# Conditioning weights by quarters, the normalised input scaled in two column parts, and the first key head one block behind the gates

## The chip, the cores and the metric

The kernel runs on one core of one Trainium2 chip. A core has a matrix engine (TensorE, PE in the profile; its weight loads are listed as PEld), VectorE (DVE), ScalarE (ACT), GpSimd (POOL) and SyncE (SP), which here only starts transfers. The metric is device microseconds of one execution; shown are the median and the spread of three.

## The reference

A two-layer backbone over 512 latent tokens and 256 context tokens with 1024 channels. Layer 0 is a bidirectional gated DeltaNet, layer 1 attention. All that matters here is how layer 0 begins:

```
shift, scale, gate = jnp.split(sc_lat @ ada_w[i] + ada_b[i], 3, axis=-1)      # and the same for the context
u_lat = rms_norm(h_lat, norm_g[i]) * (1.0 + scale[:, None]) + shift[:, None]
p = u @ w_in
```

`ada_w[0]` is 1024 by 3072: its first third of columns gives the shift, the second the scale, the last the gate. Channel block k (128 channels of the 1024) of u needs shift and scale of that block alone. The product `u @ w_in` runs over all eight channel blocks. Its columns hold queries, keys, values, a gate path, and 64 columns called `ab`, from which the recurrence's gates are made.

## The kernel before

The first 60 us are one stage in which TensorE, VectorE and ScalarE follow an order written out by hand (`tc.manual_schedule`); within it a scheduler may place instructions from later code in gaps, and it orders the transfers, which SyncE issues one after another from one queue.

The stage works as follows.

Six tiles of x (two of context, four latent; 128 tokens by 1024) are loaded, squared and summed on ScalarE (L325), and once all six sums are there and one reciprocal root is made, each tile is multiplied by its factor, alternately on VectorE (L329) and ScalarE (L331).

The conditioning weights come in blocks of 512 columns, each as two loads of 1 MB (`ada_load`, L236; rows of 2 KB). Blocks 0 and 2 are the first halves of shift and scale, 1 and 3 the second halves. Five buffers take these loads, so that the sixth waits for the first products. `ada_products` multiplies a block on TensorE (L245) and copies the result to `rows` (L246). `ada_cols` turns half of the channels, shift and scale together, into columns (L258) and makes the factors `au` in two VectorE operations (L262, L263).

`turn_x(k)` turns channel block k of all six tiles on TensorE (L341), into the two PSUM buffers of the tag "tr". `make_u(k)` multiplies by scale and adds shift: the context part on VectorE (L353), the latent part on ScalarE (L355). It then splits u in a high part (ScalarE cast, L358) and the remainder (VectorE, L359). `gemm_step(nm, ..., k)` adds block k's three products (high by high, low by high, high by low) for context and latents to the sums of `nm` (L228): once for `ab`, once for the first key head `k0`. Called a gate step and a key step here, they take 1.05 us each at the full clock.

Weights of the projection are split likewise by `load_w`: a ScalarE cast (L210) and a subtraction (L211), on VectorE for `ab`, on GpSimd for `k0` and the later key heads. A block of these weights has two raw buffers.

The order per block k was: make u(k), turn block k+1, gate step k, key step k. The products of block 1 come ahead of that at k = 1, those of block 3 at k = 2, the second columns at k = 3. Behind the stage the first key head's convolution, the gates and the other key heads follow in the scheduler's order, and later stages in the order of a planner that the change doesn't touch.

## Time and profile before

| what | value |
| --- | --- |
| median of three runs | 1182.38 us (1180.96 to 1186.59) |
| the profiled execution's own time | 1193.88 us |
| its span | 1192.1 us |
| TensorE busy | 1134.5 us, 95% |
| VectorE busy | 836.9 us, 70% |
| ScalarE busy | 705.8 us, 59% |
| GpSimd busy | 631.4 us, 53% |
| TensorE busy in the first 60 us | 38.6 us |

The profile comes from one execution, slower than the median by about 1%; differences of times are taken within it. A line of the timeline gives start and duration in us, the engine, the line of the kernel, the operation, output and inputs with partitions by elements, the count, and in brackets how long the engine stood idle before it and what ended that. A line of the chain of waits gives start, duration and what the end hung on. A line by stretch gives, after the stretch and its length, the busy time of PE, PEld, DVE, ACT and POOL with their counts of instructions, TensorE's granted clock (1.00 is full), the DMA engines' busy share and GB/s.

### The profile page before, as it was taken

The page shows a single profiled execution, that of the slowest core. Times are in us where ns is not written, and L with a number is a line of the kernel's source. Part 1 is how long each engine was busy: PE and PEld are TensorE (multiplying, and loading weights), DVE is VectorE, ACT ScalarE, POOL GpSimd, SP SyncE. Part 2 cuts the span into 40 slices and gives each one's busy share as a digit, 9 for nine tenths or more (in the row PEclk, how much of TensorE's full clock was granted, in tenths as well). Part 3 has the DMA queues.
Part 4 walks back from the last instruction along what each step waited for, and adds up shares of the span by engine and source line. Part 5 has one row for each costly group of instructions (what it writes and reads, how often), then busy time and mean ns, then how long its engine had stood idle before and what let it go on. Part 6 is the DMA issues. An engine that isn't in the chain of part 4 may idle for free.

```text
span 1192.1 us, 28134 instructions
## 1 busy us (share of the span) xinstructions
PE 1134.5 (95%) x10779; PEld 921.5 (77%) x10779; DVE 836.9 (70%) x1842; ACT 705.8 (59%) x1831; POOL 631.4 (53%) x515
## 2 busy tenths in 40 slices
PE   3999999999998999999999999999998989999996
PEld 1777678888887888888566666788886878989885
DVE  2498664778889687777678888687667866556536
ACT  5544344677666668655779888653533246666632
POOL 0031014329999899793575598557663043153531
PEclk9999999999999999999999999999999999999999
DMA  9478977555646585785988856576743021121133
GB/s 320 167 229 243 305 238 207 152 170 143 175 118 206 186 237 176 238 255 172 276 225 243 248 155 172 169 228 191 234 159 124 1 71 36 37 71 37 40 131 77
DMA packets 166104, 204.56 MB, mean 172 GB/s; under 512 B 13489, under 2 KB 115026, under 8 KB 165202
## 3 DMA queue, kind: packets, MB, share of 16 engines
q1 hardware_dynamic: 159170, 199.13, 55.0%
q10 hardware_dynamic: 6800, 3.64, 1.0%
q8 instruction: 85, 1.39, 0.5%
q14 instruction: 49, 0.40, 0.1%
HBM read 161.96 MB, written 40.67 MB: 170 GB/s over the span
## 4 chain that ended last, share of the span: by engine, by line
PE 82%; DVE 6%; DMA 6%; ACT 2%; issue 2%; SPq 1%; POOL 1%; ACTq 0%; DVEq 0%; POOLq 0%
PE g L752 29%; PE po L1385 11%; PE ks L1460 6%; PE pg L2026 3%; PE pg L1980 3%; PE g_k L414 3%; PE po L2094 2%; DMA aw<-in_ada_w 2%; PE kv L1833 2%; PE su L1515 2%; PE s L2044 2%; PE pso L2327 2%; PE pr L1485 2%; PE pa L245 1%; PE pt L2072 1%
## 5 line engine op out<-in xcount | busy, mean ns | idle before, releaser
L752 PE MATMUL g<-uh,wh 128*128 128x512 f32 (+1 forms) x640 | 222.0, 347 | 0.0
L752 PE MATMUL g<-ul,wh 128*128 128x512 f32 (+1 forms) x640 | 217.7, 340 | 3.9 <-issue 3.9
L752 PE MATMUL g<-uh,wl 128*128 128x512 f32 (+1 forms) x640 | 217.1, 339 | 0.0
L769 DVE SCALAR_TENSOR_TENSOR acc<-g,cwv,acc 128x510 f32<-128x510 f32 (+1 forms) x192 | 117.0, 614 | 43.7 <-ACT acc L761 39.2
L752 PEld LDWEIGHTS g<-uh,wl 128*128 128x128 f32 x640 | 122.8, 192 | 17.4 <-issue 4.2
L752 PEld LDWEIGHTS g<-uh,wh 128*128 128x128 f32 x640 | 122.8, 192 | 14.6 <-issue 1.1
L752 PEld LDWEIGHTS g<-ul,wh 128*128 128x128 f32 x640 | 123.0, 192 | 12.5 <-issue 0.5
L1385 PE MATMUL po<-woh,y 128*128 128x512 f32 x384 | 127.7, 400 | 0.0
L1468 POOL TENSOR_TENSOR S<-S,glb 128x512 f32<-128x512 f32 x88 | 89.9, 1041 | 58.1 <-PE ks L1460 58.1
L1052 POOL TENSOR_TENSOR X<-X,tmp 128x62 f32<-128x62 f32 (+15 forms) x93 | 95.6, 1028 | 7.3
L1051 POOL TENSOR_TENSOR tmp<-L,X 128x62 f32<-128x62 f32 (+15 forms) x93 | 94.6, 1018 | 6.4
L1460 PE MATMUL ks<-S,ckq 128*64 128x256 f32 x768 | 93.5, 386 | 2.3 <-ACT O L1465 2.2
L1385 PEld LDWEIGHTS po<-woh,y 128*128 128x128 f32 x384 | 72.2, 188 | 14.8 <-issue 0.2
L1460 PEld LDWEIGHTS ks<-S,ckq 128*64 128x64 f32 x768 | 51.1, 137 | 41.5 <-ACT O L1465 10.4
L1328 POOL TENSOR_TENSOR wol<-wo,woh 128x512 fp32r<-128x512 f32 (+1 forms) x32 | 52.6, 1643 | 56.2 <-ACT woh L1319 25.5
L1385 PE MATMUL po<-wol,y 128*128 128x512 f32 x192 | 75.1, 391 | 0.0
L743 POOL TENSOR_TENSOR wl<-w,wh 128x1024 fp32r<-128x1024 f32 x11 | 26.4, 2399 | 90.5 <-ACT wh L738 72.8
L211 POOL TENSOR_TENSOR wl_k<-w_k,wh_k 128x1024 fp32r<-128x1024 f32 x8 | 19.0, 2386 | 99.2 <-ACT wh_k L210 99.2
L761 ACT ACTIVATE acc<-g,cwv 128x512 f32<-128x512 f32 (+1 forms) x48 | 27.9, 581 | 64.2 <-PE g L752 63.7
L2075 DVE TENSOR_TENSOR pT<-pt,pT 128x384 fp32r<-128x384 f32 x64 | 33.4, 554 | 45.4 <-ACT pT L2074 45.4
L1463 DVE SCALAR_TENSOR_TENSOR r<-ks,negV,cv 128x128 f32<-128x128 f32 x192 | 56.6, 345 | 7.2 <-PE ks L1460 3.6
L1533 DVE TENSOR_TENSOR S<-su,S 128x512 f32<-128x512 f32 x88 | 56.6, 685 | 5.7 <-PE su L1515 3.9
(416 smaller groups left out, 2887.8 us busy)
## 6 DMA issues: line engine op xcount, KB each, us to landing
aw<-in_ada_w SPq DMA_DIRECT2D x24, 1024.0 KB, 7.5
w<-in_dn_w_in SPq DMA_DIRECT2D x40, 512.0 KB, 4.9
wo<-in_dn_w_out SPq DMA_DIRECT2D x32, 512.0 KB, 3.9
cv<-v_d SPq DMA_DIRECT2D x80, 128.0 KB, 5.5
df<-gc_d SPq DMA_DIRECT2D x48, 128.0 KB, 3.5
z_d<-sil SPq DMA_DIRECT2D x16, 384.0 KB, 4.3
v_d<-vt SPq DMA_DIRECT2D x16, 384.0 KB, 4.2
t_d<-Tt SPq DMA_DIRECT2D x6, 1024.0 KB, 4.7
```

Of the source, the lines that this page charges most:

```text
L414: mm = T.matmul(pg_[:m, :n], w[:, k, :m], u[:, k, c0:c0 + n], start=k == 0 and n_ == 0, stop=k == KT - 1 and n_ == 2)
L752: T.matmul(ps[:, :n], w_[:, k], u[:, k, c0:c0 + n], start=k == 0 and m == 0, stop=k == KT - 1 and m == 2)
L769: V.scalar_tensor_tensor(a_[:, c0 + lo:c0 + hi], ps[:, lo + j - 2:hi + j - 2], cwv[:, j, ct:ct + 1], a_[:, c0 + lo:c0 + hi], ALU.mult, ALU ...
L1051: G.tensor_tensor(tv, bcast(L[:, :, j + 1:, j], 3, j + 1), bcast(X[:, :, j, 0:j + 1], 2, n), ALU.mult)
L1052: G.tensor_tensor(X[:, :, j + 1:, 0:j + 1], X[:, :, j + 1:, 0:j + 1], tv, ALU.subtract)
L1328: G.tensor_tensor(wl[:, :c], w[:, :c], wh[:, :c], ALU.subtract)
L1385: T.matmul(acc[j][nh], y[i][:, j, :], ww[k][:, nh * 512:(nh + 1) * 512], start=h == 0 and x == 0, stop=h == VH - 1 and x == 2)
L1460: T.matmul(ks[r0:r0 + 64, w], kq[:, w, slot(hh), r0:r0 + 64], St[hh][:, d], start=True, stop=True)
L1463: V.scalar_tensor_tensor(r[:, 2 * j + i], ks[:, 0, i], negV[:, visit, t, h0 + i:h0 + i + 1], v[:, 2 * hh + i], ALU.mult, ALU.add)
L1468: G.tensor_tensor(St[hh], St[hh], bcast(g_, 3, P), ALU.mult)
L1533: V.tensor_tensor(St[hh], raw(sj, 0, [[512 - 1024 * j, 2], [P, 2], [1, P]]), St[hh], ALU.add)
L1980: T.matmul(pgq, uL[i][:, k, t * P:(t + 1) * P], wq[j][:, k], start=k == 0 and n_ == 0, stop=k == KT - 1 and n_ == 2)
```

## The change

First, the conditioning weights come in four quarters of 256 channels, shift and scale of a quarter as two loads of 1 MB with rows of 1 KB. The quarter's products, copy and columns follow at their own places: quarter 0 before the first turning, quarters 1, 2 and 3 within the blocks k = 1, 3 and 5. The factors are made in three VectorE operations that read PSUM. Second, each x tile is multiplied in two column parts, columns 0 to 255 at once, the rest later, between the blocks. Third, the first key head's step for block k comes after the gate step of the next block or behind the next products, so that it runs a block behind. Besides, the low part of the first key weights moves from GpSimd to VectorE, and the two constants `arow` and `dtrow` are loaded from ScalarE's queue at the start.

```diff
+        def split_high():
+            split_at[1] = S.copy(wh[:, :, :m], w[:, :, :m]).ins
+
+        def split_low():
+            split_at[0] = E.tensor_tensor(wl[:, :, :m], w[:, :, :m], wh[:, :, :m], ALU.subtract).ins
...
-        return wh, wl, split_up
+        return wh, wl, split_high, split_low
...
-        aw = {nb: ada_load(st, 0, nb) for nb in (0, 2)}
+        nc.scalar.dma_start(arow, a["dn_a_log"].rearrange("o d h -> o (d h)").partition_broadcast(P).squeeze(1))
+        nc.scalar.dma_start(dtrow, a["dn_dt_bias"].rearrange("o d h -> o (d h)").partition_broadcast(P).squeeze(1))
+
+        def ada_quarter(s):
+
+            ws = []
+            for v in range(2):
+                w = st.tile([P, KT, 256], F32, tag="aw", name=f"awq{s}{v}", bufs=5)
+                dma(w, a["ada_w"][0].rearrange("(p k) n -> p k n", k=KT)[:, :, v * D + s * 256:v * D + s * 256 + 256])
+                ws.append(w)
+            return ws
...
+        def quarter_products(s):
+
+            ps = pa.tile([P, 512], F32, tag="gq", name=f"paq{s}")
+            for v, w in enumerate(quarter.pop(s)):
+                for kh in range(2):
+                    for g in range(4):
+                        T.matmul(ps[32 * g:32 * g + 32, v * 256:v * 256 + 256], sc[:, kh * 4 + g, :], w[:, kh * 4 + g, :], start=kh == 0, stop=kh == 1, tile_position=(0, 32 * g))
+            quarter["sums", s] = ps
+
+        def quarter_rows(s):
+
+            rows = quarter["rows", s] = st.tile([P, 512], F32, tag="rows", name=f"rowsq{s}", bufs=2)
+            S.copy(rows, quarter.pop(("sums", s)))
+
+        def quarter_cols(s):
...
+            for b in range(4):
+                T.matmul(pc[:, 2 * b:2 * b + 2], rows[:, b * P:(b + 1) * P], sel[:, :, 0], start=True, stop=True)
...
+            V.tensor_tensor(pcv[:, :, 1], pcv[:, :, 1], bcast(bb[:, 1], 1, 2), ALU.add)
+            V.scalar_tensor_tensor(au[0][:, :, 1, ks], pcv[:, :, 1], 1.0, bcast(chv[:, 48 + 2 * s:50 + 2 * s], 1, 2), ALU.add, ALU.mult)
+            V.tensor_tensor(au[0][:, :, 0, ks], pcv[:, :, 0], bcast(bb[:, 0], 1, 2), ALU.add)
+
+        quarter[0] = ada_quarter(0)
         wab = load_w(w_in, 6144, 64, "ab", V, False)
-        wk0 = load_w(w_in, 8 * P, P, "k0", G, False)
+        wk0 = load_w(w_in, 8 * P, P, "k0", V, False)
+        quarter[1] = ada_quarter(1)
...
-            for t in range(NT):
-                if t % 2 == 0:
-                    V.tensor_scalar(xn[t], xn[t], ssq[:, t:t + 1], None, ALU.mult)
+
+            def scale_x(t, E, c):
+
+                if E is V:
+                    V.tensor_scalar(xn[t][:, c], xn[t][:, c], ssq[:, t:t + 1], None, ALU.mult)
                 else:
-                    S.activation(xn[t], xn[t], AF.Copy, scale=ssq[:, t:t + 1])
+                    S.activation(xn[t][:, c], xn[t][:, c], AF.Copy, scale=ssq[:, t:t + 1])
+
+            quarter_products(0)
+            early_c, late_c = slice(0, 256), slice(256, D)
+            for t in (0, 1, 2, 3, 4):
+                scale_x(t, V, early_c)
+            scale_x(5, S, early_c)
+            quarter_rows(0)
+            scale_x(0, V, late_c)
...
-            rows = [st.tile([P, 2, 512], F32, tag="rows", name=f"rows0{half}", bufs=2) for half in range(2)]
-            ada_products(0, 0, aw.pop(0), rows[0][:, 0])
             turn_x(0)
-            ada_products(0, 2, aw.pop(2), rows[0][:, 1])
             wab[2]()
-            wk0[2]()
-            aw.update({nb: ada_load(st, 0, nb) for nb in (1, 3)})
...
+            scale_x(1, S, late_c)
+            quarter[2] = ada_quarter(2)
+            quarter[3] = ada_quarter(3)
             dma(masks, a["masks"])
-            ada_cols(0, rows[0], 0)
+            quarter_cols(0)
+            wab[3]()
             gemm_open("ab")
             gemm_open("k0")
             for k in range(KT):
                 make_u(k)
+                if k == 0:
+                    wk0[2]()
+                    scale_x(2, V, late_c)
+                    wk0[3]()
                 if k == 1:
-                    ada_products(0, 1, aw.pop(1), rows[1][:, 0])
-                if k == 2:
-                    ada_products(0, 3, aw.pop(3), rows[1][:, 1])
-                if k == 3:
-                    ada_cols(0, rows[1], 1)
+                    scale_x(3, S, late_c)
+                    scale_x(4, V, late_c)
+                    scale_x(5, S, late_c)
+                if k % 2 == 0 and k > 0:
+                    gemm_step("k0", *wk0[:2], P, k - 1)
                 if k + 1 < KT:
                     turn_x(k + 1)
                 gemm_step("ab", *wab[:2], 64, k)
-                gemm_step("k0", *wk0[:2], P, k)
-                if k == 2:
+                more = k // 2 + 1 if k % 2 == 1 and k < 7 else None
+                if more:
+                    quarter_products(more)
+                    quarter_rows(more)
+                if k % 2 == 1:
+                    gemm_step("k0", *wk0[:2], P, k - 1)
+                if more:
+                    quarter_cols(more)
+                if k == KT - 1:
+                    gemm_step("k0", *wk0[:2], P, k)
+                if k == 4:
                     pv2 = pa.tile([P, 512], F32, tag="gq", name="pv2")
```

8 lines of the change are left out of this document (6 added, 2 removed).

## The prediction

> **What bounds the kernel now.** I read the page's first block, then the chain of waits over the first 120 us, the busy time by stretch, the timeline of the first 64 us instruction by instruction, and the groups by shape of the same stretch. The page:
>
> ```profile
> span 1192.1 us, 28134 instructions
> PE 1134.5 (95%) x10779; PEld 921.5 (77%) x10779; DVE 836.9 (70%) x1842; ACT 705.8 (59%) x1831; POOL 631.4 (53%) x515
> ```
>
> TensorE is the bound of the whole. The chain shows the first 60 us, the only stretch that the diff touches:
>
> ```profile
> 9.42 13.93 DMA aw<-in_ada_w
> 23.39 1.06 PE pa L245 x8
> ...
> 54.93 0.66 PE px L341 x6
> 55.59 1.03 PE g_ab L228 x6
> 56.62 1.05 PE g_k L228 x6
> ...
> 58.73 1.07 PE g_k L228 x6
> ```
>
> To 25 us it waits for conditioning weights, at the end it is pure TensorE: 0.66 us of turnings and two steps of 1.05 us (gates, first key head) per block of 128 columns. The last step ends at 59.8. What follows decides whether a shift there reaches the end:
>
> ```profile
> 60.00:70.00 10.00, 10.00 (x73) 8.52 (x70) 9.08 (x18) 5.45 (x11) 4.42 (x2) 1.00 1.03 335
> 70.00:80.00 10.00, 10.00 (x82) 7.39 (x82) 9.79 (x29) 4.35 (x7) 2.40 (x1) 1.00 0.49 138
> 80.00:100.00 20.00, 19.79 (x146) 14.54 (x147) 19.50 (x58) 8.76 (x21) 4.26 (x2) 1.00 0.78 255
> ```
>
> The first busy column is TensorE, the third VectorE: TensorE has no slack behind the stage, so I carry a shift of the stage's end to the kernel's end in full.
>
> **The change, part by part.** The start, from the timeline:
>
> ```profile
> 2.13 0.45 ACTq L298 DMA_DIRECT2D sel<-in_sel  x1
> 3.24 1.28 ACT L316 ACT_TABLE_LOAD   x1 [3.24 <-DMA cc<-in_c_ctx]
> 7.47 1.06 ACT L325 ACTIVATE junk<-x 128x1024 f32<-128x1024 f32 x1 [0.92 <-DMA x<-in_ctx]
> ...
> 15.37 1.94 PE L245 MATMUL pa<-aw,sc 128*32 128x512 f32 x8 [10.27 <-DVE rs L189]
> 16.21 3.23 ACT L331 ACTIVATE x<-x,ssq 128x1024 f32<-128x1024 f32 x3 [2.45 <-DVE ssq L190]
> 16.21 2.08 DVE L329 TENSOR_SCALAR x<-x,ssq 128x1024 f32<-128x1024 f32 x3
> 17.99 1.58 PE L245 MATMUL pa<-aw,sc 128*32 128x512 f32 x8 [0.68 <-DMA aw<-in_ada_w]
> ...
> 24.52 0.58 ACT L246 COPY rows<-pa 128x512 f32<-128x512 f32 x1 [4.29 <-PE pa L245]
> 25.62 1.04 ACT L210 CAST wh_k<-w_k 128x1024 fp32r<-128x1024 f32 x1
> 25.66 0.69 DVE L211 TENSOR_TENSOR wl_ab<-w_ab,wh_ab 128x512 fp32r<-128x512 f32 x1 [7.37 <-ACT wh_ab L210]
> 26.65 0.17 DVE L262 TENSOR_TENSOR au<-pc,chv 128x16 f32<-128x16 f32 x1 [0.29 <-PE pc L258]
> 26.75 2.34 POOL L211 TENSOR_TENSOR wl_k<-w_k,wh_k 128x1024 fp32r<-128x1024 f32 x1 [26.31 <-ACT wh_k L210]
> 26.85 2.25 DVE L263 SCALAR_TENSOR_TENSOR au<-au,chv 128x8 f32<-128x8 f32 x1
> 29.83 1.51 PE L341 MATMUL px<-ident,x 128*128 128x128 f32 x6 [3.22 <-DVE u L353]
> ```
>
> Two constants move to ScalarE's queue: two issues of 0.45 us after the one at 2.13 end at 3.5, 0.25 us past the table load's start. It is hidden by the squares, which wait for x (0.92 us at 7.47); without that cover it costs 0.25.
>
> First quarter: as many bytes as the first old block, in its place, but in pieces of 1 KB, not 2 KB. Rates:
>
> ```profile
> 8.00:10.00 2.00, 0.00 (x0) 0.00 (x0) 0.00 (x0) 1.77 (x4) 0.00 (x0) 1.00 1.03 422
> 14.00:16.00 2.00, 0.63 (x4) 0.23 (x8) 1.67 (x10) 0.00 (x0) 0.00 (x0) 1.00 1.06 390
> 24.00:26.00 2.00, 2.00 (x22) 1.61 (x15) 0.34 (x1) 1.48 (x3) 0.00 (x0) 0.98 1.06 255
> 26.00:28.00 2.00, 0.61 (x4) 0.52 (x3) 1.67 (x3) 0.67 (x1) 1.25 (x1) 0.50 1.00 370
> 28.00:30.00 2.00, 0.17 (x1) 0.20 (x2) 1.65 (x2) 0.78 (x1) 1.08 (x1) 0.50 0.43 123
> 32.00:34.00 2.00, 2.00 (x10) 1.27 (x8) 1.43 (x4) 1.11 (x3) 0.00 (x0) 0.81 1.05 408
> ```
>
> The last column is GB/s: 422 while x moves (4 KB pieces), 390 with 2 KB, 255 with projection weights of 256 and 512 B. Per piece on one of 16 engines that is 155 and 84 ns for the first two; a line through them gives 48 ns at 1 KB, 338 GB/s: 3.1 us per MB where it was 2.7. So the second half lands at 18.8 (bounds: 18.0 if nothing is lost, 20.8 at 255 GB/s). The Trainium skill (DMA: Bandwidth & Descriptors, Specifications) names 512 B as the least size for line rate; by it the quarter lands at 18.0 and the end is 0.8 us earlier. The row at 255 has half its bytes in 512 B pieces and speaks for a loss.
>
> Durations for what comes next, from the same timeline:
>
> ```profile
> 38.93 1.07 PE L245 MATMUL pa<-aw,sc 128*32 128x512 f32 x8
> 41.78 1.05 ACT L210 CAST wh_k<-w_k 128x1024 fp32r<-128x1024 f32 x1 [3.25 <-DMA w_k<-in_dn_w_in]
> 44.66 1.95 PE L258 MATMUL pc<-sel,rows 128*128 128x2 f32 x16
> 54.77 0.82 PE L341 MATMUL px<-ident,x 128*128 128x128 f32 x6
> 55.19 0.54 DVE L353 TENSOR_SCALAR u<-px,au 128x256 f32<-128x256 f32 x1
> 55.63 0.78 ACT L355 ACTIVATE u<-px,au 128x512 f32<-128x512 f32 x1 [1.16 <-PE px L341]
> 56.30 0.91 ACT L358 CAST uh<-u 128x256 fp32r<-128x256 f32 x2
> 56.73 1.21 DVE L359 TENSOR_TENSOR ul<-u,uh 128x256 fp32r<-128x256 f32 x2 [1.00 <-ACT uh L358]
> 59.71 0.31 PEld L457 LDWEIGHTS ptab<-ident,abc 64*64 64x64 f32 x8 [0.36 <-ACT wh_k L210]
> ```
>
> The early parts of x (256 columns) cost VectorE 0.27 each and end at 17.6, x0's late part at 18.2: all under the wait for the second half, and nothing but a few tenths of us if that landed at 18.0. From there, with 0.05 us between engines and 0.1 ahead of TensorE: last products 1.07 (19.9), copy 0.58 (20.5), columns, half of the 1.95 us block, 1.0 (21.6), three small VectorE operations of 0.2 (22.25). Before, these factors stood at 29.1, of which 2.1 were lost as VectorE's 0.17 us operation took 2.25 exactly while GpSimd worked on wl_k (26.75 to 29.09); the split moves to VectorE and the new operation reads PSUM, so this stall goes. **The head start is 6.9 us.**
>
> Then in order of the new code. VectorE: wl_ab 0.69 (22.9), context u 0.54 (23.5); ScalarE's casts of u (0.91 the two) end at 24.45, VectorE's low parts at 25.2; ScalarE's cast of the key weights (1.04) ends at 25.5; x2's late columns 0.60 (25.8; 2.08/3 a tile for 1024 columns); wl_k0 at 128x1024 1.35, twice the 0.69 (27.1). It sits ahead of the second u: context u 27.1 to 27.7, ScalarE's casts to 28.65. Only behind those stand x3's and x5's late columns, 0.88 each (3/4 of 3.23/3, and 0.07 fixed): 30.4. Turning block 2 needs column 256 of every x, so TensorE stands, but for turning 1 and one gate step (2 us), **from 21.6 to 30.5**. The late x is late next: 30.5 against the old wait's end at 29.8. By then the new order is one turning and one gate step ahead, half a column block and half the products behind.
>
> The half clock of 26 to 32 (0.50, then 0.81) followed a sparse stretch like this one, so it may come again; on the work right behind 30.5 (0.44 of turning, 1.05 of gate step, taking twice as long) it costs 1.5 us if it lasts to 33, nothing if it is over. The Trainium skill (TensorE: Matmul & The Clock Gate, Part 1) lets the clock fall after an idle window of 3.4 us; by it the emptier 25.8 to 30.5 brings the half clock and the stage ends at 64.05.
>
> From the last turning (55.59) to u's last low part (57.94) pass 2.35 us. In the old order a gate step, a key step and a turning, 2.76, cover that. In the new order key steps go in pairs around the columns, so between a pair's two blocks stand only a gate step and a turning, 1.71. A pair, counted from its columns' end: key step to 1.05; factors at 0.65, context u 1.24, latent u 1.44; turning 1.34 to 2.0; casts to 2.36, low parts 2.27 and 3.10; gate step in pieces to 3.67; second context u behind the low part 3.10 to 3.64, turning 3.74 to 4.40, casts to 4.61, low parts to 5.35, gate step to 5.92; products 1.08, key step 1.05, columns 0.95: 9.0 us with 7.55 of work, **1.45 idle**. Blocks 4 and 5 carry the convolution weights' turning (0.35) and its VectorE copy, which stands ahead of a u: 10.45. Blocks 6 and 7 come to 8.0 (5.9 of work). Blocks 1 to the second columns: 0.44+1.05+1.08+1.05+0.95 = 4.6.
>
> **Sum:** 30.5+4.6+9.0+10.45+8.0 = 62.55; 64.05 with the half clock. I take the middle, 63.3, for neither row decides the clock: 3.5 behind 59.8. Off that 0.3, since the copies of the gates now lie under two key steps and the 0.36 us at 59.71 goes. Net +3.2: span 1192.1 to 1195.3. The profiled execution lies 11.5 us above the median of 1182.38 (its own time is 1193.88); I carry the difference over: **1185.6**. With hand-offs at nothing and 2 KB rates the stage ends at 60.3 (+0.3); both bounds are in the range. The last quarter's second load waits for a buffer until the second products (34.6 at the latest); behind it on SyncE may stand the next key weights, needed at 64, and that hides it.
>
> **The rivals.**
> First, *not slower*: the head start carries. If the late x come before the second u's casts end, or hand-offs are shorter than my 0.05 to 0.1 us, the work left from 30.5 without idle is 4.6+7.55+7.9+5.9 = 26.0: 56.5, with half of the 6.1 of stalls (1.45+2.55+2.1; half is 3.0) and no half clock 59.5, less 0.3: -0.6; with turning 2 at 28.5, -2.6: 1180. For it: 6.9 us of head start and the stall removed. Against: the 1.71 against 2.35, and ScalarE's place for x3 and x5.
> Second, *clearly slower*: ScalarE's cast of the next key weights is not in the hand-written order and already landed inside it at 41.78, with 3.25 us of waiting for its load. The loads are no faster now; set ahead of the third u (37.3) it holds ScalarE until 42.8, 5.5 us: 1191. Decided by whether ScalarE reaches it before the load. Against: it hid before, and there are later gaps. GpSimd's low part behind it could hold a VectorE operation for 2.3 us more.
> Third, part of the delay is swallowed: VectorE is 91 to 98% busy behind the stage; if it sets the pace there, what counts is that the gates' work begins one key step (1.05) earlier relative to TensorE: +2.1, 1184.5. Against: the gate steps themselves end later (two key steps ahead of the stage's end: 60.45 to 61.95, against 58.73).
>
> **How the numbers follow.** Forecast 0.50, first rival 0.21, second 0.13, third 0.16. I call 0.5% (5.9 us) what can be told from no change. Faster than 1176.5 needs a stage end at 53.9, below the 56.5 without idle: 0.05, a quarter of the first rival. Above 1188.3: the second rival and a tail of the forecast, 0.14. The rest, 0.81, is no change. The range takes in the first and half of the second rival: 1178 to 1190.5; the forecast's own is 1182.5 to 1187.5.
>
> **What would show it.** Right: factors ready near 22.3; TensorE idle of 4 us or more ending near 30.5 behind a scaling of x; gaps of 0.1 to 0.4 us in front of gate steps from block 2 on; last key step near 63. Wrong: turning 2 before 28, gapless blocks from 2 on, or an order after 60 us that moves by itself.

## The result, and the profile after

The changed kernel takes 1197.80 us (median of four runs, 1194.87 to 1198.48) against 1184.08 us for the kernel before (four runs, 1180.96 to 1186.59). The ratio is 1.0105 with a 95% interval of 1.0079 to 1.0131: 12.4 us slower (9.4 to 15.5); the two medians lie 13.7 us apart. Forecast were 3.2 us more, and the range ended at 1190.5.

The first lines of the page of the profile after:

```profile
span 1192.8 us, 28283 instructions
PE 1136.8 (95%) x10843; PEld 921.7 (77%) x10843; DVE 825.5 (69%) x1856; ACT 706.1 (59%) x1832; POOL 632.0 (53%) x514
```

The two spans, 1192.1 before and 1192.8 now, hide the loss: the profiled execution of the kernel before (1193.88) lies 9.8 us above the median of its timed runs, that of the changed one (1194.87) 2.9 below its median. How much of that lies behind the stage shows in the run d_exp below: its later code is that of before, the row shown next stands within 0.2 us of its place there, and its span is 1184.3. So the comparison is made inside the traces, at the end of the stage and at one row of later, unchanged code. That row, from the timeline of ScalarE, before and after:

```profile
252.29 0.47 ACT L761 ACTIVATE acc<-g,cwv 128x256 f32<-128x256 f32 x1 [0.98 <-PE g L752]
```

```profile
263.47 0.47 ACT L829 ACTIVATE acc<-g,cwv 128x256 f32<-128x256 f32 x1 [0.98 <-PE g L820]
```

The changed kernel is 11.2 us late there, about what the timed runs say. It is already late by that much when the stage ends (71.00 in place of 59.78). That the two numbers agree is partly luck: between the stage's end and that row TensorE waits 3.35 us in the changed kernel and 1.17 us before, and for the same 1500 matmuls it is busy 189.1 us in place of 191.3.

The timeline of the changed kernel's stage (start, duration, engine, line, operation, in brackets the idle time ahead and what ended it):

```profile
2.63 0.44 ACTq L311 DMA_DIRECT2D arow<-in_dn_a_log  x1
2.79 3.66 SPq L309 DMA_DIRECT2D x<-in_x  x4
3.46 0.34 ACTq L312 DMA_DIRECT2D dtrow<-in_dn_dt_bias  x1
...
13.85 1.06 ACT L373 ACTIVATE junk<-x 128x1024 f32<-128x1024 f32 x1 [0.16 <-DMA x<-in_x]
...
19.81 1.93 PE L331 MATMUL paq<-awq,sc 128*32 128x256 f32 x16 [0.97 <-DMA awq<-in_ada_w]
...
24.38 0.15 DVE L350 TENSOR_TENSOR au<-pcq,chv 128x4 f32<-128x4 f32 x1
...
25.46 0.88 PE L399 MATMUL px<-ident,x 128*128 128x128 f32 x6 [1.40 <-ACT u L413]
...
30.26 1.76 ACT L381 ACTIVATE x<-x,ssq 128x768 f32<-128x768 f32 x2
...
31.24 1.30 PE L399 MATMUL px<-ident,x 128*128 128x128 f32 x3 [1.32 <-ACT x L381]
...
34.39 3.12 PE L331 MATMUL paq<-awq,sc 128*32 128x256 f32 x32
...
38.60 0.95 PE L344 MATMUL pcq<-sel,rowsq 128*128 128x2 f32 x8
...
40.16 1.05 ACT L216 CAST wh_k<-w_k 128x1024 fp32r<-128x1024 f32 x1 [1.98 <-DMA w_k<-in_dn_w_in]
...
41.28 2.35 POOL L217 TENSOR_TENSOR wl_k<-w_k,wh_k 128x1024 fp32r<-128x1024 f32 x1 [40.84 <-ACT wh_k L216]
...
42.21 2.31 DVE L417 TENSOR_TENSOR ul<-u,uh 128x256 fp32r<-128x256 f32 x2 [1.60 <-ACT uh L416]
...
43.97 0.48 PE L234 MATMUL g_ab<-ul,wh_ab 128*64 128x256 f32 x1 [1.26 <-DVE ul L417]
...
48.20 1.93 PE L331 MATMUL paq<-awq,sc 128*32 128x256 f32 x32
...
51.21 0.95 PE L344 MATMUL pcq<-sel,rowsq 128*128 128x2 f32 x8
...
62.26 0.95 PE L344 MATMUL pcq<-sel,rowsq 128*128 128x2 f32 x8
...
70.61 0.39 PE L234 MATMUL g_k<-uh,wl_k 128*128 128x512 f32 x1
```

The last key step ends at 71.00, where it ended at 59.78. The rows to keep in mind are the start (x's issues take 3.66 us), the scaling of x at 30.26 with TensorE waiting behind it, and the cast at 40.16, which belongs to the next key head and stands between the third factors and the third u.

In the kernel before, the same issue and the last square:

```profile
2.80 1.83 SPq L303 DMA_DIRECT2D x<-in_x  x4
...
12.61 1.06 ACT L325 ACTIVATE junk<-x 128x1024 f32<-128x1024 f32 x1 [0.15 <-DMA x<-in_x]
```

Last, busy time by stretch of the changed kernel (PE, PEld, DVE, ACT, POOL, then granted clock, DMA share, GB/s):

```profile
24.00:26.00 2.00, 0.60 (x6) 0.54 (x6) 1.46 (x5) 1.16 (x3) 0.00 (x0) 1.00 1.09 348
26.00:28.00 2.00, 1.92 (x10) 0.97 (x7) 1.84 (x4) 2.00 (x4) 0.00 (x0) 0.65 1.11 341
...
34.00:36.00 2.00, 2.00 (x18) 0.79 (x20) 0.00 (x0) 0.00 (x0) 0.00 (x0) 0.50 1.09 348
36.00:38.00 2.00, 2.00 (x24) 1.07 (x17) 0.00 (x0) 0.41 (x1) 0.00 (x0) 0.79 1.12 338
...
44.00:46.00 2.00, 2.00 (x7) 1.36 (x8) 1.43 (x4) 0.93 (x2) 0.00 (x0) 0.50 0.46 111
```

By the shares of the mixed stretches (0.65 is 0.6 us at full and 1.4 at half) the clock is halved from about 26.6 to 36.8, and a second time in a spell that holds all of 44 to 46 (43.7 to 47.1 by stretches of 1 us); before, it was halved once, from 26 to 32.8.

One thing this column doesn't show. It lists 1.00 from the start, but the first products of the stage run at half speed: 16 instructions take 1.93 us at 19.81, where 32 take 1.93 at 48.20, and in the kernel before 8 take 1.94 at 15.37 and 1.07 at 38.93. In the changed kernel full speed comes at about 23 us. Ahead of the first halving the clock is therefore read from the durations.

### The profile page after: what moved, and what is told of

It is laid out like the page before. It is cut to its first block, busy times and chain, and to the rows that moved or that the text cites. A ratio compares the mean times of both kernels' runs of the same rounds, so it can differ in the third digit from the quotient of the medians.

```text
span 1192.8 us, 28283 instructions
## 1 busy us (share of the span) xinstructions
PE 1136.8 (95%) x10843; PEld 921.7 (77%) x10843; DVE 825.5 (69%) x1856; ACT 706.1 (59%) x1832; POOL 632.0 (53%) x514
## 4 chain that ended last, share of the span: by engine, by line
PE 74%; POOL 7%; DVE 7%; DMA 6%; ACT 3%; issue 2%; SPq 1%; POOLq 0%; ACTq 0%; DVEq 0%
PE g L820 21%; PE po L1453 11%; PE ks L1528 6%; PE pg L2094 3%; PE pg L2048 3%; PE g_k L482 3%; PE su L1583 2%; POOL tmp L1119 2%; PE po L2162 2%; PE kv L1901 2%; PE s L2112 2%; POOL X L1120 2%; PE pr L1553 2%; PE pso L2395 2%; PE pq L1575 1%
## 5 line engine op out<-in xcount | busy, mean ns | idle before, releaser
L1119 POOL TENSOR_TENSOR tmp<-L,X 128x62 f32<-128x62 f32 (+15 forms) x93 | 98.8, 1063 | 6.4
L217 POOL TENSOR_TENSOR wl_k<-w_k,wh_k 128x1024 fp32r<-128x1024 f32 x7 | 16.8, 2404 | 117.9 <-ACT wh_k L216 117.9
L2167 POOL TENSOR_TENSOR yT<-ay,yT 128x256 fp32r<-128x256 f32 x16 | 11.8, 738 | 91.3 <-ACT yT L2166 91.3
```

What stands on the lines that cost most here:

```text
L1119: G.tensor_tensor(tv, bcast(L[:, :, j + 1:, j], 3, j + 1), bcast(X[:, :, j, 0:j + 1], 2, n), ALU.mult)
```

## The experiments

Each run is judged by three numbers: where the last key step of the stage ends, how far the later ScalarE row (252.29 in the kernel before) has moved, and the ratio of the timed runs. The first two come from one trace each; the ratio's interval is about 0.2 to 0.5% to each side; so what differs by a few us at the stage's end cannot always be told apart in the ratio.

| run | last key step ends | later row moves | ratio, 95% interval |
| --- | --- | --- | --- |
| before | 59.78 | 0 | 1 |
| changed | 71.00 | +11.2 | 1.0105 (1.0079 to 1.0131) |
| a_const_back | 71.44 | +8.2 | 1.0108 (1.0060 to 1.0155) |
| a_no_hoist | 67.90 | +11.5 | 1.0103 (1.0058 to 1.0148) |
| a_whole_x | 69.42 | +7.3 | 1.0103 (1.0065 to 1.0142) |
| a_key_not_behind | 75.97 | +15.9 | 1.0153 (1.0108 to 1.0198) |
| a_fill | 71.00 | +9.0 | one time, 1192.95 us |
| a_fill_cast_held | 66.58 | +4.3 | 1.0081 (1.0050 to 1.0111) |
| a_three_undone | 63.41 | +2.0 | 1.0034 (1.0008 to 1.0059) |
| b_quarters | 64.88 | +4.8 | 1.0051 (1.0020 to 1.0082) |
| b_key_behind | 60.92 | -2.4 | 0.9975 (0.9953 to 0.9998) |
| b_low_on_V | 61.49 | +1.4 | 0.9988 (0.9959 to 1.0016) |
| b_const_early | 60.02 | +1.0 | 1.0002 (0.9982 to 1.0021) |
| c_low_const | 67.60 | +7.5 | 1.0040 (1.0023 to 1.0057) |
| c_low_const_fill | 66.43 | +6.6 | 1.0082 (1.0051 to 1.0114) |
| d_exp | 59.73 | -0.2 | 1.0013 (0.9992 to 1.0034) |
| d_key_exp | 60.91 | -2.4 | 0.9988 (0.9962 to 1.0015) |
| d_low_key_exp | 60.37 | -2.7 | 0.9984 (0.9963 to 1.0006) |

Names with a_ are the changed kernel with parts taken back or added, the others the kernel before with parts of the change.

### One part taken back at a time

The two constants back on SyncE's queue:

```diff
-        nc.scalar.dma_start(arow, a["dn_a_log"].rearrange("o d h -> o (d h)").partition_broadcast(P).squeeze(1))
-        nc.scalar.dma_start(dtrow, a["dn_dt_bias"].rearrange("o d h -> o (d h)").partition_broadcast(P).squeeze(1))
...
+            dma(arow, a["dn_a_log"].rearrange("o d h -> o (d h)").partition_broadcast(P).squeeze(1))
+            dma(dtrow, a["dn_dt_bias"].rearrange("o d h -> o (d h)").partition_broadcast(P).squeeze(1))
             dma(masks, a["masks"])
```

> The changed kernel with the two constants arow and dtrow back on SyncE's queue, where they were (ahead of the masks). In the changed kernel the issue of the four latent x tiles took 3.66 us where it took 1.83, the DMA engines stood half idle from 6 to 8 us, and the last square started at 13.85 instead of 12.61. Theory: two issues on ScalarE's queue with 128 pieces of 128 B each hold up SyncE's. Then the last square is back at 12.6, the scaling of x starts at 16.2 instead of 17.45, and the last key step ends 1.2 us earlier than 71.0. Rival: the 1 KB pieces behind x fill the queue; then x stays at 13.85 and the stage's end does not move.

Measured, the timeline's rows of the same two places:

```profile
2.81 2.09 SPq L309 DMA_DIRECT2D x<-in_x  x4
...
12.88 1.06 ACT L371 ACTIVATE junk<-x 128x1024 f32<-128x1024 f32 x1
```

x is back by 1.0 us, and the late scaling ends at 30.84 in place of 32.02. The stage's end does not follow (71.44): the clock is then halved from 25.3 to 35.5 and again from 42.3 to 49.2, and the next key head's casts stand in the third u as before.

The later key heads' casts held back until the stage's last cast of u:

```diff
         def split_up():
-            split_at[1] = S.copy(wh[:, :, :m], w[:, :, :m]).ins
+            with tc.issue_after(last_cast[0]):
+                split_at[1] = S.copy(wh[:, :, :m], w[:, :, :m]).ins
...
-                    S.copy(uh[:, k, c0:c0 + w_], u32[:, :w_])
+                    last_cast[0] = S.copy(uh[:, k, c0:c0 + w_], u32[:, :w_]).ins
```

> The changed kernel with the later key heads' weight casts on ScalarE held behind the stage's last cast of u, so that none is placed inside the stage. Theory: in the changed kernel the cast at 40.16 waited 1.98 us for its load and took 1.05, GpSimd's low part behind it held VectorE's low part of u for 1.1 us, and TensorE's clock fell again from 44 to 47; without it the stage ends 2 to 3.5 us earlier than 71.0, at 67.5 to 69. Against that the second key head's weights are ready only after the stage: its first product may start up to 2 us behind the last key step. Rival, the chain of u alone sets the blocks' pace: under 1 us gained.

The timeline's rows of the third u's low part, and of a later cast:

```profile
41.08 1.21 DVE L419 TENSOR_TENSOR ul<-u,uh 128x256 fp32r<-128x256 f32 x2 [0.56 <-ACT uh L418]
...
77.56 1.05 ACT L218 CAST wh_k<-w_k 128x1024 fp32r<-128x1024 f32 x1 [1.46 <-DMA w_k<-in_dn_w_in]
```

The low part takes 1.21 again, not 2.31, the two blocks from the second columns' end to the third's take 9.59 us in place of 12.61 with the clock full throughout, and the stage ends 3.1 us earlier. But two raw buffers serve all key heads: what is cast late frees its buffer late, and the fourth key head's weights wait for their load until 77.56 (their cast is at 70.81 in the changed kernel, where GpSimd is done with the buffer at 43.6 and the load is issued at 43.66; here it is issued from 67.78 on). The later row stands at +11.5: between 88 us and that row TensorE waits 3.7 us for a VectorE operation on the gates and 2.5 us for later conditioning weights. So the gain is given back behind the stage; that the late buffer brings these waits about is likely, but not shown.

x scaled whole, all of it ahead of the first turning's use:

```diff
-            early_c, late_c = slice(0, 256), slice(256, D)
-            for t in (0, 1, 2, 3, 4):
-                scale_x(t, V, early_c)
-            scale_x(5, S, early_c)
+            for t in range(NT):
+                scale_x(t, S if t % 2 else V, slice(0, D))
```

> The changed kernel with every x tile scaled at once, as before, instead of in two column parts. Theory: VectorE and ScalarE stood idle from 19 to 22 us, so the whole scaling costs nothing there, and TensorE no longer waits for late columns until 31 to 32: turning 2 starts near 28, the stage ends 2.5 us earlier than 71.0 from that alone, 4 us with less of the half clock. Rival, the half clock is set by the sparse stretch before it and the chain of u by its own latency: under 1 us.

The third turning starts at once at 28.5 and the clock is full again from 30.2 (36.8 in the changed kernel), but the cast now falls into the third u at 40.31, and TensorE stands 1.79 and 2.07 us behind it. 1.6 us are left of the gain.

The key step right behind its gate step again:

```diff
-                if k % 2 == 0 and k > 0:
-                    gemm_step("k0", *wk0[:2], P, k - 1)
...
-                if k % 2 == 1:
-                    gemm_step("k0", *wk0[:2], P, k - 1)
+                gemm_step("k0", *wk0[:2], P, k)
...
-                if k == KT - 1:
-                    gemm_step("k0", *wk0[:2], P, k)
```

> The changed kernel with the first key head's step right behind the gate step of the same block, as before. The prediction's step says that key steps in pairs leave the chain of u uncovered, 1.45 us a pair and 6.1 in all; if that is the cause, the stage ends 3 to 5 us earlier than 71.0. Rival: with the factors coming by quarters the wait only moves in front of the gate step behind each quarter's columns, where nothing is left to cover it; then the end is within 0.8 us of 71.0, and the gate steps end about 1 us later than the 68.8 of the changed kernel.

The view of waits of TensorE over this run's stage (in all, times, longest):

```profile
PE px L399 <- DVE u L411: 4.2, 4, 1.2
PE g_ab L234 <- DVE ul L417: 1.9, 1, 1.9
```

It is 5.0 us worse, which neither the theory nor the rival had, and the clock is halved three times (39.7 to 49.9, 56.8 to 60.2, 70.4 to 73.8). The wait of 1.9 is the next head's cast again. With quarters there are four columns, and behind each the chain of factors, u and PSUM buffer stands open for 1.2 us unless a key step lies over it. So the key head a block behind is no loss in this order, it covers part of a loss that the quarters bring.

### Two covers of one loss

Full clock by 24 added transposes in TensorE's empty places; their result isn't used:

```diff
             quarter_cols(0)
+            fill(8)
...
                 gemm_step("ab", *wab[:2], 64, k)
+                if k == 0:
+                    fill(16)
```

> The changed kernel with 24 idle turnings of x's first block added on TensorE where it stood idle, 8 behind the first quarter's columns and 16 behind the first gate step; their result is not used. Theory of the clock: the half clock from 27 to 37 comes from the sparse stretch ahead of it; with the filler the granted clock stays at 1.00 there, and the last key step ends 2 to 4 us earlier than 71.0 in spite of the added work. Rival: the clock falls all the same, or the waits set the pace whatever the clock; then the end stays or moves later by up to 2 us.

TensorE is at half speed until about 27.6 and at full speed from there to 44.8 us (halved again until 48.2), and the stage ends at 71.00 to the hundredth. The timeline says why:

```profile
39.90 1.04 ACT L216 CAST wh_k<-w_k 128x1024 fp32r<-128x1024 f32 x1 [0.55 <-DMA w_k<-in_dn_w_in]
...
41.28 2.97 DVE L417 TENSOR_TENSOR ul<-u,uh 128x256 fp32r<-128x256 f32 x2 [2.17 <-ACT uh L416]
...
43.71 0.33 PE L234 MATMUL g_ab<-ul,wh_ab 128*64 128x256 f32 x1 [2.07 <-DVE ul L417]
```

Everything arrives 1.5 us earlier and waits for the cast, which waits for its load, which lands at about 40 whatever TensorE does; then GpSimd's low part (41.02 to 43.37) holds VectorE's. Both treated at once, with the casts held only until the fourth block's casts of u:

```diff
             with tc.issue_after(last_cast[0]):
                 split_at[1] = S.copy(wh[:, :, :m], w[:, :, :m]).ins
...
                 if k == 3:
                     last_cast[0] = cast.ins
```

> The changed kernel with both suspects treated at once: 24 transposes more, whose result nobody reads, in TensorE's empty places of the stage (as in the run with the filled gaps, where the clock stayed at 1.00 until 44 us and the stage's end did not move from 71.0), and ScalarE's casts of the later key heads held until the fourth block's casts of u. Constants, column parts of x and the key head a block behind stay as the change has them. Theory, clock and cast are two covers of one loss, and each alone leaves the other in place: the last key step ends at 64.5 to 67, and the kernel lies at 1.003 to 1.007 of the kernel before. Rival, the cast is the only thing and the clock costs nothing: 67.9, as with the cast held alone. Second rival, a load that lands late sets the pace whatever is done: still 69.5 to 71.

66.58: 4.4 us, where the filled gaps alone brought none and the held cast alone 3.1. The theory holds for the stage; for the whole (1.0081, expected 1.003 to 1.007) it was too hopeful.

Constants, x whole and the cast held, all three, quarters and the order of the change kept:

```diff
-        nc.scalar.dma_start(arow, a["dn_a_log"].rearrange("o d h -> o (d h)").partition_broadcast(P).squeeze(1))
...
-            early_c, late_c = slice(0, 256), slice(256, D)
...
+                scale_x(t, S if t % 2 else V, slice(0, D))
...
+            with tc.issue_after(last_cast[0]):
+                split_at[1] = S.copy(wh[:, :, :m], w[:, :, :m]).ins
```

> The changed kernel with three things undone at once: the constants back on SyncE's queue, every x tile scaled whole, and the second key head's cast held until the fourth block's casts of u (not until the stage's end, which took 3.4 us back later by delaying the next weights). Quarters, the key head a block behind and the low part on VectorE stay. Theory: the terms add up; the stage ends at 62.5 to 65 (71.0 in the changed kernel, 59.8 before), the whole is 5 to 8 us below the changed kernel and still 2 to 5 us above the kernel before, since the blocks wait for each quarter's columns. Rival: quarters themselves gain, and the end is at or below 59.8.

63.41. TensorE runs at half speed until about 30.4, by the durations of its matmuls, and at full speed from there to the stage's end. Taken back alone, the three move the stage's end by -0.4, 1.6 and 3.1 us (4.3 in all), together by 7.6: each was standing in front of another. Where the 3.6 us left come from is the question of the runs below.

### Parts of the change on the kernel before

Quarters alone, the rest as before:

```diff
-        aw = {nb: ada_load(st, 0, nb) for nb in (0, 2)}
+        quarter[0] = ada_quarter(0)
...
+        quarter[1] = ada_quarter(1)
```

> The kernel before with the quarters alone: x scaled whole, key step right behind the gate step, key low part on GpSimd ahead of the columns, constants on SyncE. Theory: columns four times instead of twice, each in front of two blocks, cost more than the earlier first factors give: the stage ends at 63 to 66 (59.8 before). Rival: the quarters are the gain and the other parts the loss: 55 to 59.

```profile
PE px L394 <- DVE u L406: 5.4, 5, 1.2
```

That row of TensorE's waits holds one wait behind each of the four columns (23.5, 34.8, 45.0, 57.1) and one of 0.57. The kernel before has 3.22 and 0.48 us of waits behind its first columns, so the waits are only a part of the 5.1 us; one more quarter's products (1.93) lie behind the first columns, the clock is halved once more, from 58.7 to 62.1, and the rest isn't told apart. In the order before there were two columns, and the second came a block ahead of its need, with a gate step and a key step over it.

The low part of the key weights on VectorE, behind the first u:

```diff
-        wk0 = load_w(w_in, 8 * P, P, "k0", G, False)
+        wk0 = load_w(w_in, 8 * P, P, "k0", V, False)
...
+                if k == 0:
+                    wk0[3]()
```

> The kernel before with one thing of the change: the first key weights' low part on VectorE behind the first u, not on GpSimd ahead of the factors. Theory: VectorE's factor operation no longer stands 2.1 us behind GpSimd; factors at 27.0 instead of 29.1, the stage ends 1.5 to 2.2 us earlier than 59.8, the whole 1.5 to 2 us below the kernel before. Rival: the added 1.2 us on VectorE delays the second block's u by as much, or the half clock lasts longer; under 0.8 us.

```profile
30.74 0.23 ACT L518 ACTIVATE arow<-arow 128x32 f32<-128x32 f32 x1 [2.87 <-DMA arow<-in_dn_a_log]
...
31.32 0.47 PE L234 MATMUL g_ab<-uh,wh_ab 128*64 128x256 f32 x1 [2.01 <-ACT uh L364]
```

The factors stand at 27.07, 2.0 us earlier, and nothing comes of it: an exponential of a constant row, placed between u and its casts, waits for its load.

Nor can the 2.0 us be put down to the move. In the run with the key head behind (below) GpSimd has the low part ahead of the factors, as before:

```profile
26.77 0.17 DVE L263 SCALAR_TENSOR_TENSOR au<-au,chv 128x8 f32<-128x8 f32 x1
26.95 2.35 POOL L211 TENSOR_TENSOR wl_k<-w_k,wh_k 128x1024 fp32r<-128x1024 f32 x1 [26.50 <-ACT wh_k L210]
```

The factor operation takes 0.17, for it is done when GpSimd begins. It is so in b_const_early, d_exp and d_key_exp too. In the trace of the kernel before VectorE waited 0.29 us for the first columns, which took 2.22 us in place of 1.95, since the clock had fallen during them; in the four others it waited for nothing. So GpSimd began at 26.75, ahead of that operation at 26.85. The stall of 2.1 us is thus a matter of a tenth of a microsecond in one execution, not a property of the kernel; where it is missed, u's first low part can meet GpSimd's instead (2.13 in place of 1.21 in d_exp).

Moving those loads behind the squares on ScalarE's queue was meant to mend the wait for the row, and with 16 added transposes, whose result isn't used, to keep the clock up:

```diff
             rsqrt(ssq, 1.0 / D)
+            nc.scalar.dma_start(arow, a["dn_a_log"].rearrange("o d h -> o (d h)").partition_broadcast(P).squeeze(1))
+            nc.scalar.dma_start(dtrow, a["dn_dt_bias"].rearrange("o d h -> o (d h)").partition_broadcast(P).squeeze(1))
...
+            fill(6)
```

> The kernel before, with its two whole-block loads and x scaled whole, and two edits: the low part of the first key weights on VectorE behind the first u (in place of GpSimd), and the two constant rows on ScalarE's queue behind the squares of x, so that the exponential of the first row does not wait for its load between u and u's casts (2.87 us of wait with the low part moved alone, where the last key step ended at 61.49). Theory, the stall removed is worth what the factors gain once nothing new waits: factors near 27.1, no wait for the row, last key step at 57.5 to 58.5, kernel at 0.997 to 0.9995. Rival, the longer emptiness in front of the third half block brings the half clock for longer and eats it: last key step at 59.5 to 61, kernel at 0.999 to 1.002.

> The same two edits, and 16 transposes more whose result nobody reads, in TensorE's empty places around the second half block's products and behind the first columns, to keep the clock up. Theory, the half clock of 26 to 32 us is the rest of the loss: granted clock 1.00 from 24 on, last key step at 55.5 to 57.5, kernel at 0.995 to 0.999. Rival, the transposes themselves stand ahead of products that are due, or the loads of the weights set the stage's pace: last key step at 58 to 61, kernel at 0.999 to 1.003.

Both missed altogether. ScalarE's timeline of the first:

```profile
23.58 0.35 ACTq L333 DMA_DIRECT2D arow<-in_dn_a_log  x1
24.31 0.36 ACTq L334 DMA_DIRECT2D dtrow<-in_dn_dt_bias  x1
24.72 3.23 ACT L339 ACTIVATE x<-x,ssq 128x1024 f32<-128x1024 f32 x3 [10.75 <-DMA w_ab<-in_dn_w_in]
```

The first issue, due behind the last square (14.0), went out at 23.58, and ScalarE's scaling of x, whose factors stood at 16.4, began at 24.72; the trace puts the wait down to the landing of the `ab` weights. The stage ended at 67.60 and 66.43. These runs say nothing of the theory, but much of what an issue on a computing engine's queue can cost. The same two loads at the start, where the change has them, and nothing else:

> The kernel before with the loads of the two constant rows moved to ScalarE's queue at the start, as the change has them, and nothing else. Theory: SyncE's four issues of the latent tiles of x take 3.0 to 3.7 us in place of 1.83, the last square ends 1.0 to 1.3 us later (13.6 to 13.9), and since the first columns wait for weights the factors come 0 to 1.2 us later: last key step at 59 to 61, kernel at 0.999 to 1.002. Rival (what the prediction costed): hidden by the squares, last square at 12.6, and the exponential, whose row is there, waits for nothing: last key step at 58.5 to 59.8, kernel at 0.998 to 1.000.

```profile
2.79 3.44 SPq L303 DMA_DIRECT2D x<-in_x  x4
...
14.24 1.06 ACT L327 ACTIVATE junk<-x 128x1024 f32<-128x1024 f32 x1
```

SyncE's four issues take 3.44 in place of 1.83 and the last square starts 1.6 us later; the factors come at 28.36, earlier than the 29.10 of the kernel before only because they miss the 2.1 us described above. The stage's end moves by 0.24, the whole by nothing that can be measured. In the order before, then, an x late by 1.6 us is covered.

The key step a block behind, in the order before:

```diff
-                gemm_step("k0", *wk0[:2], P, k)
+                if k:
+                    gemm_step("k0", *wk0[:2], P, k - 1)
+                if k == KT - 1:
+                    gemm_step("k0", *wk0[:2], P, k)
```

> The kernel before with one edit: the first key head's step runs one block of 128 columns behind the gates' step. The run that took this part out of the changed kernel ended 5.0 us later, so there it covers the chain from turning to u's low part. Theory, in the order of before that chain is covered already (no idle time in front of gate steps from 54.9 on), so nothing is to be had: last key step at 59.5 to 60.1, gates' last step 1.0 us earlier (57.7), kernel at 0.9985 to 1.001. Rival, the key step behind fills the idle that stands ahead of the first gate step too: last key step at 57 to 59 and the kernel at 0.996 to 0.9985.

```profile
249.89 0.47 ACT L764 ACTIVATE acc<-g,cwv 128x256 f32<-128x256 f32 x1 [0.98 <-PE g L755]
```

The last key step ends 1.1 later, the gates' last step 0.1 later (58.83), and the later row stands 2.4 us earlier. From the stage's end to that row TensorE is busy 188.97 us without a wait, where the kernel before has 191.34 us for the same matmuls and 1.17 of waits; 2.3 of the difference lie in the products of later conditioning weights (L245: 16.8 in place of 19.1). That this comes from the gates' sums, complete a key step before the end, is a reading that no run isolates. Neither theory had that place. At 0.9975 this kernel looks slightly faster than the one before, and so than both; its interval only just leaves out 1, and d_key_exp below, with the same two numbers, has 0.9988 and an interval that holds 1.

Three more on the same ground, with the exponential held behind the fourth block's casts: alone, with the key head behind, and with the low part on VectorE besides.

```diff
-    S.activation(arow, arow, AF.Exp)
+    with tc.issue_after(last_cast[0]):
+        S.activation(arow, arow, AF.Exp)
```

> The kernel before with the exponential held behind the fourth block's casts of u, and nothing else. Theory: in the kernel before the factors come late (29.1) for the 2.1 us that GpSimd's low part holds VectorE, and the row's load lands at about 30.7, so the exponential costs at most 0.5 to 1.5 us there: last key step at 58.3 to 59.8, kernel at 0.9975 to 1.0005. Rival: nothing stands behind the exponential in this order, last key step at 59.8 within 0.1.

> The kernel before with the key head's step a block behind, and the exponential held behind the fourth block's casts; the low part stays on GpSimd. With the key head behind alone the factors stood at 26.9, but u's casts waited behind the exponential until 31.1. Theory: first gate step at 28.5 to 29.5 in place of 31.5, last key step at 58 to 59.5, kernel at 0.993 to 0.997. Rival: the factors fall back to 29.1 (VectorE's operation held by GpSimd's low part, as in the kernel before), and the hold gains nothing: first gate step at 31.5, kernel at 0.996 to 0.9995.

> The kernel before (whole-block weights, x scaled whole, constants on SyncE's queue) with the order of the change otherwise: low part of the first key weights on VectorE behind the first u, key head's step a block behind the gates' step; and ScalarE's exponential of a constant row held behind the fourth block's casts of u, so that it cannot stand between u and its casts. It is the changed kernel with three parts taken back, less the quarters. Theory, the quarters are what is left of the loss (+5.1 alone; +3.6 with these two parts): last key step at 57 to 60, gates' last step at 55 to 58, kernel at 0.993 to 0.998 of the kernel before. Rival, the order itself costs: last key step at 62 to 64, kernel at 1.002 to 1.005.

The hold alone ends within 0.1 of the kernel before, as its rival said; the other two end at 60.91 and 60.37, later than their theories had it.

In the last of them the first gate step begins at 28.01, 3.0 us ahead of the trace of the kernel before, and the clock is full from 32 on. It has whole blocks in place of quarters, and its stage ends at 60.37, its gates at 58.27, where the run with three parts taken back has 63.41 and 61.30: **the 3 us left come with the quarters.** Three smaller things differ besides. The key steps follow one by one, where the quarters' columns make them go in pairs; the exponential is held only here, which alone moves nothing; the next head's cast is held only there, but in neither run does a gate step wait for it. Quarters and pairs are not told apart by these two runs. But the stage doesn't end earlier than before either. Its timeline shows the bound:

```profile
33.76 1.06 PE L252 MATMUL pa<-aw,sc 128*32 128x512 f32 x8 [1.69 <-DMA aw<-in_ada_w]
...
40.00 1.07 PE L252 MATMUL pa<-aw,sc 128*32 128x512 f32 x8 [1.27 <-DMA aw<-in_ada_w]
```

The last conditioning weights are there at 40.0; in the kernel before and in b_key_behind, b_const_early, d_exp and d_key_exp their products wait for them too and begin between 40.4 and 40.7. From there to the end it is TensorE's work. The 3 us gained ahead are waited away in front of these loads (1.69 and 1.27). None of the three is measurably faster than the key head behind alone.

What the quarters, with the key steps in pairs, do to a gate step shows in two pairs of rows, first and last of one step's six, in the run with three parts taken back (third block):

```profile
36.77 0.36 PE L236 MATMUL g_ab<-uh,wh_ab 128*64 128x256 f32 x1
...
38.14 0.40 PE L236 MATMUL g_ab<-uh,wl_ab 128*64 128x512 f32 x1
```

and in the one with whole blocks (sixth block; its third takes the same):

```profile
52.14 0.36 PE L235 MATMUL g_ab<-uh,wh_ab 128*64 128x256 f32 x1
...
53.03 0.39 PE L235 MATMUL g_ab<-uh,wl_ab 128*64 128x512 f32 x1
```

1.37 from first to last start against 0.89: the step comes in pieces, as u's low parts get ready. The six steps of blocks 2 to 7 (counted from 0) take 8.5 us together against 5.3, which is 3.2 us.

## Why the prediction was wrong, and where it was right

The sign was right; the size was not, and anything above 1188.3 had been given only 0.14. Its stage was 30.5 + 4.6 + 9.0 + 10.45 + 8.0 = 62.55. The trace, by the ends of the columns (39.55, 52.16, 63.21) and the late x at 32.02, has 32.02 + 7.53 + 12.61 + 11.05 + 7.79 = 71.00. The 8.45 us between are 1.5, 2.9, 3.6, 0.6 and -0.2. The steps that failed, in the order of their size, are the second rival's cast, which was left out of the sum (3.0 in the third term), the quarters' products, priced at one load for two (0.85 in each of three terms), the half clock (about 2.1 in the second term), and the constants called hidden (1.2 in the first term); the rest of the working was 0.4 too long. Step by step:

- **Late x, 30.5.** The mechanism was right: TensorE waits for a scaling of x on ScalarE. It ended 1.5 later, and 1.2 of that is the step "two constants move to ScalarE's queue ... hidden by the squares". The prediction costed ScalarE's own time (0.25) and looked at no other queue; what was paid is SyncE's, whose issues doubled (1.83 to 3.66). With the loads back the late scaling ends 1.2 earlier (30.84). The run with this move alone shows the like, 3.44 and the late square, though there it costs the kernel nothing.
- **"Last products 1.07" and "products 1.08".** Mis-sized, measured 1.93. The row of 1.07 is one load of 1 MB; a quarter has two, and the row of the kernel before that holds two says so:

```profile
34.17 1.92 PE L245 MATMUL pa<-aw,sc 128*32 128x512 f32 x16
```

That is 0.85 too little in every one of three later quarters. Ahead of the first factors the 1.07 was meant for the second load alone, and it took 1.93 for another reason: it ran at half speed, as the 1.94 and 1.58 for one load each in the prediction's own rows at 15.37 and 17.99 could have told. These 0.86 us, a landing 1.0 later (19.81 for 18.8; 18.79 with the constants back) and a turning that went ahead of the columns brought the first factors at 24.53, not 22.25. The rate of 338 GB/s for pieces of 1 KB was good: 341 and 348 in the stretches above.
- **Half clock, 0 to 1.5.** It came, sooner and for longer, from 26.6 to 36.8: the second quarter's products took 3.12 in place of 1.93, and of the 2.9 us by which the blocks to the second columns exceed 4.6, 0.85 are the products' size, 1.2 their half clock, and the rest, about 0.9, lies in the gate step, which took 2.27 at half clock, less what had been turned before. A second spell, 43.7 to 47.1, lies in the next pair and goes when the cast is held. The prediction took a middle between two ends where it had no row; the upper end was too low, since the spell ended only at 36.8, when TensorE had been without a gap since 31.2. How much of that is luck the last section says.
- **A pair in 9.0.** Measured 12.61. The run with three parts taken back has 9.61 for the same pair (columns' ends 34.97 to 44.58), 11.03 for the next and 7.80 for the last: the working with its uncovered chain from turning to low part held within 0.6, and that is the missing 0.85 less a little. The other 3.0 are the **second rival**, the hoisted cast, at the place named, the third u: with the casts held and all else as in the changed kernel the pair takes 9.59, and the second half-clock spell is gone. Its price was put at 5.5 by a load landing at 41.8, and it landed at 40.16. "GpSimd's low part behind it could hold a VectorE operation for 2.3 us more" came too: 2.31 in place of 1.21.
- **"Key steps go in pairs", so the chain lies open.** Half right. It does lie open, but only together with the quarters: with whole blocks and the key head behind, where the key steps needn't go in pairs, gate steps are whole (0.89). With quarters, putting each key step right behind its gate step costs 5.0 more. The prediction compared with the old order and never priced the wait behind each of four columns, 1.2 us, which the key steps cover.
- **The head start of 6.9 us, the removed stall in it.** 4.6 came (24.53 in place of 29.10), and the late x used it up, as the prediction had it. But 2.1 of the 6.9 were that one execution's, as four other traces show. And in the order before nothing could have been had from it: there is a second bound at 40 us, the landing of conditioning weights. The prediction saw it neither as a bound nor as a rival; in the trace of the kernel before it is the idle of 0.48 at 40.48, so small because the stall had used up the rest.
- **The third rival** pointed at the right place: with the key head behind, 2.4 us are gained behind the stage, by a way that isn't shown. In the changed kernel TensorE's work there shrinks by about as much (189.1 for 191.3), but its waits grow by 2.2. So the shift of the stage's end was carried to the later row in full by luck, and not since TensorE had no slack there.

The cases were weighed as if one of them would come true. They came together. The clock fell before TensorE waited for the late x (26.6 against 29.9), and in the run with x whole it fell too, at 26.8, but came back at 30.2; so the late x lengthens the half clock and doesn't bring it. The third u then meets a load that lands near 40 us: at full clock ahead of it (39.90), with x whole (40.31), and in the changed kernel (40.16). The Trainium skill (SBUF - State Buffer, the two separate sides) says that VectorE's operation with two SBUF inputs and GpSimd exclude each other for a whole instruction; the trace agrees (GpSimd's low part runs from 41.28 to 43.63, and VectorE's, begun at 42.21, ends at 44.52, which leaves 0.9 us behind GpSimd of its usual 1.21). The moved low part of the first key head removed that at 27 us, and VectorE met it at 42 with the next head's.

Not settled: how the 7.6 us that three parts bring together divide among them. They cover each other, and the single runs give an order of undoing, not shares. Nor are quarters and key steps in pairs told apart, or the way by which a key head behind shortens TensorE's work after the stage.

## What to carry to other kernels

Before a gain ahead of a wait is counted, look for the next thing that arrives at a fixed time, a load above all: with whole blocks, three runs (the ones with the exponential held) that brought the first gate step 3 us forward all met the same load at 40 us. A constant's load moved to another engine's queue has two prices, the other queues' issues and that engine's computation behind it, and both are read in the rows of the issues, not in their bytes. Where undoing one part brings nothing, undo two before calling it harmless. And before a stall in one trace is counted as a gain, look at how narrowly it came about: the 2.1 us behind GpSimd hung on 0.1 us, and a second trace of nearly the same kernel doesn't have them.

## What the runs showed of the hardware that was not expected

Two small loads issued from ScalarE at 2.63 and 3.46 us, between SyncE's issues of x, lengthened these from 1.83 to 3.66 us in the changed kernel and to 3.44 with that move alone; with the loads back, 2.09. An issue from ScalarE due at 14.0 went out at 23.58. The trace names a load's landing for that wait; in the same trace an issue of SyncE that began at 19.87 was done at 23.36, 0.2 us ahead. Which of the two it was wasn't tried.

The clock fell in the changed kernel at about 26.6 us, with no idle stretch of TensorE longer than the 1.40 us up to 25.46 in the five us ahead of it, and it held through a gap of 1.69 us in d_low_key_exp (32.07 to 33.76; the products behind it take 1.06, as at full clock). The Trainium skill (TensorE: Matmul & The Clock Gate, Part 1) ties the fall to an idle window of about 3.4 us; no such window precedes it here, so by this trace a thin mixture of short gaps can suffice, and need not.

The gap of 1.40 us in the run with three parts taken back says nothing of this, although 1.00 is listed there: TensorE was still at half speed, and the same six turnings take 1.54 behind the gap where they take 0.88 in the changed kernel.

```profile
24.66 1.54 PE L396 MATMUL px<-ident,x 128*128 128x128 f32 x6 [1.40 <-ACT u L410]
```

Within a trace the changes of the clock keep a step of 3.41 us. By stretches of 1 us they lie at 26.62, 36.86, 43.68 and 47.1 us in the changed kernel, which are 3, 2 and 1 steps apart, and at 25.26, 35.50, 42.32 and 49.16 with the constants back, 3, 2 and 2 steps. Where the steps begin differs from trace to trace. So it is partly luck in which of them a sparse stretch falls, and a difference of one step between two runs' half-clock spells need not come from their edits.
